# Attention scores as two 128-row matmuls, and the head of the expert layers on VectorE alone

## The chip, the cores and the metric

The kernel runs on one core of a Trainium2 chip. A core has five engines that run side by side and wait for each other through semaphores: TensorE (PE in the profile, with PEld for the loading of its stationary operand), VectorE (DVE), ScalarE (ACT), GpSimd (POOL) and SyncE (SP), which here only starts transfers. The metric is the time of one execution on the device, in microseconds (us), lower is better; the median of three executions before the change is 2091.71 us (2089.07 to 2093.18).

## What is computed

Two blocks run one after the other on one sequence of 256 rows of 1024 values. The change touches only the first block, two layers of attention and routed experts:

```python
def first_block(x, ...):
    for layer in range(2):
        mixed = mixer_dilated(x, ...) if layer == 0 else mixer_stick_breaking(x, ...)
        x = layer_norm(ALPHA * x + mixed, ln1_g[layer], ln1_b[layer])
        ffn = moe_ffn(x, router_w, router_b, exp_w_gate[layer], ...)
        x = layer_norm(ALPHA * x + ffn, ln2_g[layer], ln2_b[layer])

def moe_ffn(x, ...):
    scores = sigmoid(x @ router_w)                       # 16 experts in 4 groups
    biased = (scores + router_b).reshape(T, 4, 4)
    group_score = top_k(biased, 2)[0].sum(-1)            # the two best of a group
    best_group = argmax(group_score, axis=-1)            # one group for each token
    ...                                                  # its two best experts, gates
    y = sum over experts of gate * (silu(x @ w_gate[e]) * (x @ w_up[e])) @ w_down[e]
```

Both attentions have 16 heads of 64 values. The dilated one has three sets of q, k and v and a softmax over each; the other ("stick-breaking") has one set, a logarithm and a running sum instead of the softmax. The second block (feed-forward, a mixture of four mixers, feed-forward, twice) is unchanged.

## The kernel before

**Two-part numbers.** A matmul takes its operands in a rounded format. To keep accuracy, the kernel splits nearly every operand into a high and a low part (`split`, lines 235 to 237: ScalarE copies to the rounded format, VectorE subtracts) and adds three products (`mm3`, lines 239 to 243). Weights come as pieces of 128 by 1024 (`raw`), are split into `whi` and `wlo`, and go to TensorE.

**Attention scores.** For a score, q·k over 64 values, `stack_q` (line 535) puts the high part of q in 64 partitions of the tile `qs` and the low part in the other 64. `stack_k` (line 542) copies the high part of k into both halves of `ks` (ScalarE, then a GpSimd copy, line 547), and writes the low part of k to half the partitions of another tile, `kl` (VectorE, line 546). `score` (line 549) issues two products into one sum: all 128 partitions of `qs` with `ks` (high·high and low·high at once), then 64 partitions of `qs` with `kl`. `dilated` (line 564) runs 8 pairs of heads; `project` makes q, k, v of a pair while `attention` of the pair before it is worked off piece by piece, 4 units (2 heads, 2 blocks of rows) with 3 scores each, over 128 or 256 keys. `stick` (line 666) runs 8 pairs with `project(hp)`, `weights(hp - 1)`, `values(hp - 2)` in each round, 4 scores for each round and head pair.

**The head of an expert layer.** `attention_out` (line 427) forms the output of attention for the two blocks of 128 rows (c = 0 and 1), normalizes each (`layer_norm`, line 407) and makes the router's logits. For c = 1 the normalization's last steps go to ScalarE (line 422) and GpSimd (line 423). `moe` (line 830) then chooses the group of each token with small VectorE steps: `sc`, `bi` (lines 852, 853), the six pair sums `pr` (line 859), maxima `gs`, `gx`, `val`, `vx` and the choice `og` (line 872). TensorE counts tokens of each group (`og` with `ones_r` and `tri_r`), VectorE takes the largest count `ci` and each token's `rank`, and `places` (line 1017) makes the 0/1 matrix `P`. `xparts` (line 1020) splits x into `xsh` and `xsl`, with GpSimd doing the subtractions (argument True of `split`). `gather(k)` (line 895) multiplies P with a piece of 128 columns of x, so that each group's tokens stand together; `XTh` and `XTl` (lines 914, 915) take the result out of PSUM. After gather(0) all engines load `ci` and branch (lines 903, 904): the long body of `overflow` runs only where a group has more than 128 tokens, and is jumped over here. Then follow gather(1) to gather(7) and `experts` (line 767), 16 experts with 3 MB of weights each.

**What sets the order.** A scheduler places the instructions of each engine, by the order of the program and its own estimates; `manual_schedule` holds an engine to the written order, `issue_after` holds a piece of the program back until a given instruction. Pieces of the first expert's weights are split by `ready = list(self.parts(raws[0, 0], (2, 3)))` (line 893): pieces 2 and 3 on GpSimd.

Of the kernel before, what the change touches and what calls it, by code (L numbers as in the profile page):

```python
# [165 lines left out]
class Net:  # L166
# [240 lines left out]
    def layer_norm(self, z, gb, y, pin=False, pool=False):  # L407
# [10 lines left out]
        for s in self.halves:  # L418
            keep(nc.vector.scalar_tensor_tensor(out=y[:, s], in0=z[:, s], scalar=m[:, 0:1], in1=gb[0][:, s], op0=OP.subtract, op1=OP.mult))
        for s in self.halves:  # L420
            if pool:
                nc.scalar.activation(y[:, s], y[:, s], AF.Copy, scale=m[:, 2:3])
                self.end = nc.gpsimd.tensor_tensor(out=y[:, s], in0=y[:, s], in1=gb[1][:, s], op=OP.add)
            else:
                self.end = nc.vector.scalar_tensor_tensor(out=y[:, s], in0=y[:, s], scalar=m[:, 2:3], in1=gb[1][:, s], op0=OP.mult, op1=OP.add)
                keep(self.end)
# [58 lines left out]
    def toeplitz(self, pool, dr):  # L485

        nc = self.nc
        rel = pool.tile([32, 16], F32, name="rel", bufs=1)
        oh = pool.tile([32, 384], F32, name="oh", bufs=1)
# [4 lines left out]
        f = pool.tile([16, 384], F32, name="relf", bufs=1)  # L494
# [65 lines left out]
    def dilated(self, c1):  # L560
        nc, A = self.nc, self.A
        with self.tc.tile_pool(name="dil", bufs=1) as sp, self.tc.tile_pool(name="dr", bufs=1, space=bass.MemoryType.DRAM) as dr:
# [17 lines left out]
            def project(hp, out):  # L580
                qs, ks = (sp.tile([128, 3, 2, 256], F32R, name=n, bufs=2) for n in ("qs", "ks"))
                kl = sp.tile([128, 3, 256], F32R, name="kl", bufs=2)
                v = sp.tile([128, 2, 384], F32, name="v", bufs=2)
                out += [qs, ks, kl, v]
                for g in range(3):
                    w = w0 if hp == g == 0 else self.wload(A["dqk"][hp, g])
                    for s in range(2):
                        p = self.psB()
                        self.proj_b(p[:, :256], w[s], 0, 128, xT)
                        if s == 0:  # L590
                            self.stack_q(p, qs[:, g], lambda t: halves(t)[:, :, ::-1], halves)
                        else:
                            self.stack_k(p, ks[:, g], kl[:, g])
# [12 lines left out]
            def scores(hp, hh, qt, qs, ks, kl):  # L606
# [5 lines left out]
                for g in range(3):  # L612
                    self.score(pv[:, g, :n], qs[:, g], ks[:, g], kl[:, g], hh, q, n)
                s = sp.tile([128, 768], F32, name="s", bufs=2)
                mx = sp.tile([128, 4], F32, name="mx", bufs=4)
# [7 lines left out]
            def attention(hp, qs, ks, kl, v):  # L623
# [3 lines left out]
                for i in range(6):  # L627
                    if i < 4:
                        ready.append(scores(hp, *units[i], qs, ks, kl))
                        yield  # L630
# [39 lines left out]
    def stick(self, x):  # L670
        nc, A = self.nc, self.A
        with self.tc.tile_pool(name="sb", bufs=1) as sp:
# [25 lines left out]
            def project(hp):  # L698
                w = self.wload(A["sqk"][hp])
                qs, ks = (sp.tile([128, 2, 256], F32R, name=n, bufs=3) for n in ("qs", "ks"))  # L700
                kl = sp.tile([128, 256], F32R, name="kl", bufs=3)
                for s in range(2):
# [4 lines left out]
                    else:  # L707
                        self.stack_k(p, ks, kl)
# [7 lines left out]
                return qs, ks, kl  # L716

            def weights(qs, ks, kl):

                ps = [self.psA()[:, :384] for _ in range(2)]  # L720
                for hh, t in enumerate(ps):
                    self.score(t[:, :256], qs, ks, kl, hh, slice(128, 256), 256)
                    self.score(t[:, 256:], qs, ks, kl, hh, slice(0, 128), 128)
# [106 lines left out]
    def moe(self, x, l):  # L830
# [3 lines left out]
        with self.tc.tile_pool(name="moe", bufs=1) as sp, self.psum(512) as self.pa:  # L834
# [17 lines left out]
            v.tensor_scalar(sc, sc, 0.5, 0.5, op0=OP.mult, op1=OP.add)  # L852
# [915 lines left out]
```

## Time and profile before

| | |
|---|---|
| median of three executions | 2091.71 us |
| the profiled execution, and its span | 2091.95 us, 2090.2 us |
| PE busy | 1989.7 us (95%) |
| DVE busy | 1398.5 us (67%) |
| ACT busy | 1060.3 us (51%) |
| POOL busy | 200.6 us (10%) |
| dilated attention | about 0 to 326 us |
| head of the first and second expert layer | about 354 to 383 and 689 to 715 us |
| stick-breaking attention | about 540 to 660 us |

The profile records one execution with a start and a duration of every instruction. A busy PE is not one that works at its peak: two matmuls in a row overlap, and the time from one's start to the next one's start says more than the duration of one. The granted clock of TensorE is given as a share of full speed: 1.0 is 2.4 GHz, 0.5 is 1.2 GHz.

### The profile page before, as it was taken

To read this page: it belongs to the slowest core of one execution; us is meant where nothing else is said; L and a number is where in the kernel's file an instruction comes from. 1 tells how busy PE (TensorE), PEld (TensorE's weight loads), DVE (VectorE), ACT (ScalarE), POOL (GpSimd) and SP (SyncE) were. 2 spreads that over 40 slices of the span, in tenths; PEclk is the share of its full clock that TensorE was granted. 3 is DMA by queue.
4 is the path that set the end of the run, shared out by engine and by line. 5 is a ranking of instruction groups with operands and counts; after the bars stand their busy time and mean duration, and the time that the engine had idled before them with its cause. 6 is when DMAs were issued, how large, how long until landed. Compare 5 with 4: busy or idle time off the path is not lost. (4 is left out here: it accounts for less than half of the span.)

```text
span 2090.2 us, 38200 instructions
## 1 busy us (share of the span) xinstructions
PE 1989.7 (95%) x15106; PEld 1756.7 (84%) x15106; DVE 1398.5 (67%) x2521; ACT 1060.3 (51%) x2014; POOL 200.6 (10%) x243
## 2 busy tenths in 40 slices
PE   8999997899899699899998999999999999999998
PEld 7999996677787577699987887999899878988997
DVE  6667666788787788875566666555655576646554
ACT  5555554577565477554461334444544442335443
POOL 1212222000121200000003100000000021010000
PEclk9999998899999799999999999999999999999999
DMA  8334334698433698655543222555555543215553
GB/s 282 121 122 152 122 122 151 242 327 315 143 129 101 230 326 299 223 194 190 183 161 107 83 81 99 194 187 186 182 187 187 172 145 94 92 61 164 189 182 111
DMA packets 102528, 357.21 MB, mean 171 GB/s; under 512 B 11888, under 2 KB 15136, under 8 KB 102208
## 3 DMA queue, kind: packets, MB, share of 16 engines
q1 hardware_dynamic: 97584, 341.70, 48.8%
q10 hardware_dynamic: 4704, 12.81, 1.9%
q8 instruction: 121, 1.98, 0.4%
q14 instruction: 71, 0.58, 0.1%
q0 software_dynamic: 48, 0.13, 0.0%
HBM read 353.53 MB, written 1.07 MB: 170 GB/s over the span
## 5 line engine op out<-in xcount | busy, mean ns | idle before, releaser
L237 DVE TENSOR_TENSOR wlo<-raw,whi 128x512 fp32r<-128x512 f32 (+2 forms) x1038 | 768.3, 768 | 391.5 <-ACT whi L236 387.4
L236 ACT ACTIVATE whi<-raw 128x512 fp32r<-128x512 f32 (+2 forms) x1046 | 665.1, 667 | 607.1 <-issue 203.5
L241 PE MATMUL psB<-xTh,whi 128*128 128x256 f32 x1792 | 508.4, 284 | 8.9 <-ACT whi L236 8.3
L243 PE MATMUL psB<-xTh,wlo 128*128 128x256 f32 x1792 | 506.0, 282 | 0.2 <-DVE wlo L237 0.2
L242 PE MATMUL psB<-xTl,whi 128*128 128x256 f32 x1792 | 505.5, 282 | 0.7 <-DVE xTl L237 0.6
L241 PEld LDWEIGHTS psB<-xTh,whi 128*128 128x128 f32 x1792 | 338.8, 189 | 16.4 <-ACT whi L236 8.5
L242 PEld LDWEIGHTS psB<-xTl,whi 128*128 128x128 f32 x1792 | 339.1, 189 | 5.7 <-DVE xTl L237 1.8
L243 PEld LDWEIGHTS psB<-xTh,wlo 128*128 128x128 f32 x1792 | 339.5, 189 | 1.4 <-DVE wlo L237 0.7
L243 PE MATMUL psA<-whi,hl 128*128 128x512 f32 x352 | 139.8, 397 | 0.0
L241 PE MATMUL psA<-whi,hh 128*128 128x512 f32 x352 | 138.7, 396 | 0.0
L242 PE MATMUL psA<-wlo,hh 128*128 128x512 f32 x352 | 138.4, 393 | 0.0
L241 PE MATMUL psA<-xTh,whi 128*128 128x256 f32 (+1 forms) x352 | 105.9, 302 | 0.4 <-ACT vt L528 0.4
L241 PE MATMUL psB<-whi,XTh 128*128 128x512 f32 x256 | 103.6, 405 | 0.0
L243 PE MATMUL psA<-xTh,wlo 128*128 128x256 f32 (+1 forms) x352 | 103.3, 294 | 0.0
L242 PE MATMUL psA<-xTl,whi 128*128 128x256 f32 (+1 forms) x352 | 102.3, 291 | 0.7 <-DVE xTl L237 0.7
L243 PE MATMUL psB<-whi,XTl 128*128 128x512 f32 x256 | 101.1, 395 | 0.0
L242 PE MATMUL psB<-wlo,XTh 128*128 128x512 f32 x256 | 100.9, 394 | 0.0
L237 DVE TENSOR_TENSOR dlo<-raw,dhi 128x1024 fp32r<-128x1024 f32 (+1 forms) x68 | 80.3, 1188 | 19.5 <-ACT dhi L236 18.9
L241 PE MATMUL psB<-whi,xTh 128*128 128x384 f32 (+2 forms) x256 | 90.1, 352 | 3.3 <-ACT xTh L236 1.5
L243 PE MATMUL psB<-whi,xTl 128*128 128x384 f32 (+2 forms) x256 | 88.2, 345 | 0.3 <-DVE xTl L237 0.3
L242 PE MATMUL psB<-wlo,xTh 128*128 128x384 f32 (+2 forms) x256 | 87.9, 344 | 0.0
L292 POOL TENSOR_TENSOR ss<-ss,mh 128x1 f32<-128x1 f32 x14 | 9.5, 679 | 786.2 <-DVE ss L291 781.4
(431 smaller groups left out, 3455.3 us busy)
## 6 DMA issues: line engine op xcount, KB each, us to landing
raw<-in_egu_dram SPq DMA_DIRECT2D x128, 512.0 KB, 8.0
raw<-in_ffn1gu_dram SPq DMA_DIRECT2D x88, 512.0 KB, 3.7
raw<-in_ffn2gu_dram SPq DMA_DIRECT2D x88, 512.0 KB, 3.7
raw<-in_edn_dram SPq DMA_DIRECT2D x64, 512.0 KB, 6.7
raw<-in_dqk_dram SPq DMA_DIRECT2D x46, 512.0 KB, 3.8
raw<-in_ffn1dn_dram SPq DMA_DIRECT2D x44, 512.0 KB, 3.6
raw<-in_ffn2dn_dram SPq DMA_DIRECT2D x44, 512.0 KB, 3.7
raw<-in_wb_dram SPq DMA_DIRECT2D x40, 512.0 KB, 3.8
```

The lines of the kernel that those rows point to most:

```text
L236: self.hi = self.nc.scalar.activation(hi, src, AF.Copy)
L237: return (self.nc.gpsimd if pool else self.nc.vector).tensor_tensor(out=lo, in0=src, in1=hi.bitcast(F32), op=OP.subtract)
L241: mm(out, a[0], b[0], start=start, stop=False)
L242: mm(out, a[0], b[1], start=False, stop=False)
L243: mm(out, a[1], b[0], start=False, stop=stop)
L292: nc.gpsimd.tensor_tensor(out=ss[:, 3:4], in0=ss[:, 2:3], in1=self.mh[:, :1], op=OP.pow)
```

## The change

Scores: `ks` gets a second plane, for the low part of k. VectorE writes it where ScalarE wrote the high part, one GpSimd copy takes both planes to the other 64 partitions, and `score` issues two products over all 128 partitions with the same `qs`. `kl` is gone; the second product now holds low·low as well.

Head: the second half of `layer_norm` for c = 1 is kept as two functions (`self.steps`), and `moe` calls them between its own steps, both on VectorE. `xparts` splits only c = 0; c = 1 is split half by half inside a VectorE piece with a fixed order. `split` no longer uses GpSimd there, and the splitting of the first expert's weights, now all on VectorE, is held back behind the last of these steps. Small tiles (`rel`, `oh`, `relf`, `mx`) share memory with others.

```diff
-    def layer_norm(self, z, gb, y, pin=False, pool=False):
+    def layer_norm(self, z, gb, y, pin=False, late=False):
...
+        if late:
+            self.steps = scale, shift
+        else:
+            for f in (scale, shift):
+                for s in self.halves:
+                    keep(f(s))
...
-    def stack_k(self, p, ks, kl):
+    def stack_k(self, p, ks):
+
         for h, a, b in self.lanes:
-            self.nc.scalar.activation(ks[a, h, :], p[a, :256], AF.Copy)
+            self.nc.scalar.activation(ks[a, h, 0, :], p[a, :256], AF.Copy)
         for h, a, b in self.lanes:
-            self.nc.vector.tensor_tensor(out=kl[a, :], in0=p[a, :256], in1=ks[a, h, :].bitcast(F32), op=OP.subtract)
-            self.nc.gpsimd.tensor_copy(ks[b, h, :], ks[a, h, :].bitcast(F32))
-
-    def score(self, out, qs, ks, kl, h, q, n):
-        r = self.lanes[h][1]
-        self.mm(out, qs[:, h, q], ks[:, h, :n], True, False)
-        self.mm(out, qs[r, h, q], kl[r, :n], False, True)
+            self.nc.vector.tensor_tensor(out=ks[a, h, 1, :], in0=p[a, :256], in1=ks[a, h, 0, :].bitcast(F32), op=OP.subtract)
+            self.nc.gpsimd.tensor_copy(ks[b, h, :, :], ks[a, h, :, :].bitcast(F32))
+
+    def score(self, out, qs, ks, h, q, n):
+        for i in range(2):
+            self.mm(out, qs[:, h, q], ks[:, h, i, :n], i == 0, i == 1)
...
+            xs = self.xparts(x)
...
+            with self.tc.manual_schedule(engines={mybir.EngineType.DVE}):
...
+                tt(out=ogr, in0=val, in1=vx[:, :, None].to_broadcast([128, 2, 4]), op=OP.is_equal)
+                og8 = ogr.bitcast(F32).rearrange("p c g -> p (c g)")
+                scale(h0)
...
+                self.places(P[:, 0], rank[:, 0:4])
+                self.places(P[:, 1], rank[:, 4:8])
+                shift(h0)
+                self.split(xs[1][0][:, h0], xs[1][1][:, h0], x[1][:, h0])
+                scale(h1)
+                shift(h1)
+                placed = self.split(xs[1][0][:, h1], xs[1][1][:, h1], x[1][:, h1]).ins
             Pf = P.bitcast(F32)
-            placed = self.end.ins
-            xs = self.xparts(x)
             with self.tc.issue_after(placed):
-                ready = list(self.parts(raws[0, 0], (2, 3)))
+                ready = list(self.parts(raws[0, 0]))
```

On TensorE in the dilated attention, one unit of scores over 256 keys; `psA` is the sum, `psB` the projection of the next pair. Before:

```order
L243 MATMUL psB<-xTh,wlo 128x256
L246 MATMUL psA<-ks,qs 128x256
L246 MATMUL psA<-kl,qs 128x256
L246 MATMUL psA<-ks,qs 128x256
L246 MATMUL psA<-kl,qs 128x256
L246 MATMUL psA<-ks,qs 128x256
L246 MATMUL psA<-kl,qs 128x256
L241 MATMUL psB<-xTh,whi 128x256
```

and now:

```order
L243 MATMUL psB<-xTh,wlo 128x256
L246 MATMUL psA<-ks,qs 128x256 x6
L241 MATMUL psB<-xTh,whi 128x256
L242 MATMUL psB<-xTl,whi 128x256
L243 MATMUL psB<-xTh,wlo 128x256
```

The place among the other work is the same; the six products are now of one kind.

On VectorE in the head of the first expert layer, from the choice of the group to the branch, before:

```order
L872 TENSOR_TENSOR og<-val,vx 128x8
L237 TENSOR_TENSOR dlo<-raw_3953,dhi 128x512
L879 TENSOR_REDUCE ci<-psC 1x1
L885 TENSOR_TENSOR rank<-psC,og 128x8
L1017 TENSOR_TENSOR P<-c1t,rank 128x512 x2
L237 TENSOR_TENSOR wlo<-raw_3957,whi 128x1024
L237 TENSOR_TENSOR dlo<-raw_3955,dhi 128x512 x2
L903 TENSOR_LOAD ci
L904 COMPARE_AND_BRANCH
```

and now (L420 and L423 are the two steps of the normalization):

```order
L881 TENSOR_TENSOR og<-val,vx 128x8
L420 SCALAR_TENSOR_TENSOR x<-x,ss,row 128x512
L893 TENSOR_REDUCE ci<-psC 1x1
L895 TENSOR_TENSOR rank<-psC,og 128x8
L1030 TENSOR_TENSOR P<-c1t,rank 128x512 x2
L423 SCALAR_TENSOR_TENSOR x<-x,ss,row 128x512
L237 TENSOR_TENSOR xsl<-x,xsh 128x512
L420 SCALAR_TENSOR_TENSOR x<-x,ss,row 128x512
L423 SCALAR_TENSOR_TENSOR x<-x,ss,row 128x512
L237 TENSOR_TENSOR xsl<-x,xsh 128x512
L237 TENSOR_TENSOR wlo<-raw,whi 128x512
L917 COMPARE_AND_BRANCH
```

The weights of the first and second expert (`dlo`, `wlo`) made way for the normalization and the splits of c = 1.

On VectorE behind the branch, down to the first `XTl`, before:

```order
L994 TENSOR_TENSOR cm<-bi 128x8x3
L994 TENSOR_TENSOR cm<-bi 128x8x2
L994 TENSOR_TENSOR cm<-bi 128x8
L998 TENSOR_TENSOR rk<-c1t,cm 128x8x3
L999 COPY rk<-c1t 128x8
L915 CAST XTl<-psB 128x512
```

and now:

```order
L237 TENSOR_TENSOR wlo<-raw,whi 128x512 x7
L1007 TENSOR_TENSOR cm<-bi 128x8x3
L1007 TENSOR_TENSOR cm<-bi 128x8x2
L1007 TENSOR_TENSOR cm<-bi 128x8
L1011 TENSOR_TENSOR rk<-c1t,cm 128x8x3
L1012 COPY rk<-c1t 128x8
L928 CAST XTl<-psB 128x512
```

Seven of the eight half pieces of the first expert's weights, of which four were on GpSimd and four earlier on VectorE, now stand ahead of the first `XTl`.

## Rows read from the trace of the kernel before

**Rows 1.** Busy time by stretch: span, then each engine's busy us, clock, DMA.

```profile
core 0: us, PE busy (x) PEld busy (x) DVE busy (x) ACT busy (x) POOL busy (x), PEclk, DMA share, GB/s
100.00:200.00 100.00, 100.00 (x719) 94.38 (x718) 67.35 (x139) 54.13 (x120) 20.29 (x24) 1.00 0.43 135
...
354.00:383.00 29.00, 11.94 (x36) 9.22 (x37) 20.35 (x42) 9.54 (x18) 9.84 (x8) 0.56 0.62 228
...
420.00:440.00 20.00, 20.00 (x91) 15.92 (x90) 19.21 (x21) 16.39 (x22) 0.00 (x0) 1.00 0.88 312
...
560.00:600.00 40.00, 37.22 (x271) 33.00 (x270) 36.27 (x52) 26.90 (x49) 9.00 (x9) 1.00 0.53 172
600.00:650.00 50.00, 49.00 (x331) 41.44 (x332) 37.73 (x62) 30.64 (x57) 10.17 (x12) 1.00 0.35 117
```

**Rows 2.** Timeline of TensorE in dilated attention: start, duration, engine, line, operation.

```profile
124.62 0.38 PE L246 MATMUL psA<-kl,qs 64*128 64x256 f32 x1
124.93 0.39 PE L246 MATMUL psA<-ks,qs 128*128 128x256 f32 x1
125.24 0.38 PE L246 MATMUL psA<-kl,qs 64*128 64x256 f32 x1
125.55 0.39 PE L241 MATMUL psB<-xTh,whi 128*128 128x256 f32 x1
125.77 0.28 PE L242 MATMUL psB<-xTl,whi 128*128 128x256 f32 x1
125.89 0.29 PE L243 MATMUL psB<-xTh,wlo 128*128 128x256 f32 x1
...
128.65 0.32 PE L246 MATMUL psA<-kl,qs 64*128 64x128 f32 x1
128.90 0.33 PE L246 MATMUL psA<-ks,qs 128*128 128x128 f32 x1
```

**Rows 3.** The tile kl: loading of its stationary operand, ns min/median/max.

```profile
L246 PEld LDWEIGHTS psA<-kl,qs x128: 182/183/183, 43.1 to 651.0; 64*128 64x128 f32 x128
```

**Rows 4.** Timeline of TensorE: eight transposes of 128 columns in a row.

```profile
343.95 1.03 PE L448 MATMUL psC<-c0t,x 128*128 128x128 f32 x8
```

**Rows 5.** Timeline of GpSimd in dilated attention: one copy of line 547.

```profile
136.07 0.40 POOL L547 CAST ks<-ks 64x256 fp32r<-64x256 f32 x1
```

**Rows 6.** Timelines, head of the first expert layer, from several engines.

```profile
353.58 0.22 DVE L457 SCALAR_TENSOR_TENSOR lg<-psB,ss,br 128x16 f32<-128x16 f32 x1
354.25 2.49 POOL L423 TENSOR_TENSOR x<-x,row 128x512 f32<-128x512 f32 x2 [0.83 <-ACT x L422]
356.81 3.63 DVE L859 TENSOR_TENSOR pr<-bi 128x24 f32<-128x24 f32 x3
364.55 0.15 DVE L872 TENSOR_TENSOR og<-val,vx 128x8 fp32r<-128x8 f32 x1
366.14 1.29 DVE L1017 TENSOR_TENSOR P<-c1t,rank 128x512 fp32r<-128x512 f32 x2
370.38 0.35 DVE L994 TENSOR_TENSOR cm<-bi 128x24 f32<-128x24 f32 x3 [0.61 <-DVEq L904]
374.10 0.69 DVE L915 CAST XTl<-psB 128x512 fp32r<-128x512 f32 x1 [3.19 <-PEq L904]
374.15 0.60 ACT L914 ACTIVATE XTh<-psB 128x512 fp32r<-128x512 f32 x1 [13.73 <-PEq L904]
383.09 0.40 PE L241 MATMUL psB<-whi,XTh 128*128 128x512 f32 x1
```

**Rows 7.** Timelines, head of the second expert layer.

```profile
706.97 0.69 DVE L915 CAST XTl<-psB 128x512 fp32r<-128x512 f32 x1 [1.63 <-PEq L904]
715.13 0.40 PE L241 MATMUL psB<-whi,XTh 128*128 128x512 f32 x1
```

**Rows 8.** Line 904: TensorE's two branches, ns min/median/max, first and last start.

```profile
L904 PEldq COMPARE_BRANCH  x2: 3612/4530/5448, 368.5 to 703.2; - x2
```

**Rows 9.** Busy time by stretch: the first gathers behind the branch, columns as in Rows 1.

```profile
374.10:379.40 5.30, 5.28 (x13) 4.19 (x14) 2.51 (x8) 2.39 (x4) 0.00 (x0) 0.50 0.99 389
```

More of the change, by code (lines that the diff above doesn't have):

```diff
@@ L417, in layer_norm, with scale, shift @@
         self.rstd(m[:, 1:2], m[:, 2:3], 1.0, LN_EPS)
[L418 to L426, printed above, removed]
+        def scale(s):
+            return nc.vector.scalar_tensor_tensor(out=y[:, s], in0=z[:, s], scalar=m[:, 0:1], in1=gb[0][:, s], op0=OP.subtract, op1=OP.mult)
+        def shift(s):
+            self.end = nc.vector.scalar_tensor_tensor(out=y[:, s], in0=y[:, s], scalar=m[:, 2:3], in1=gb[1][:, s], op0=OP.mult, op1=OP.add)
+            return self.end
+        if late:
[4 more added lines that the diff above has]
+                    keep(f(s))
         return m
@@ L884, in moe @@
-            rank = sp.tile([128, 8], F32, name="rank")
-            tt(out=rank, in0=rp[:, :8], in1=og8, op=OP.mult)
-            P = sp.tile([128, 2, 4, 128], F32R, name="P")
-            for c in range(2):
-                self.places(P[:, c], rank[:, c * 4:c * 4 + 4])
+            scale, shift = self.steps
+            h0, h1 = self.halves
+            with self.tc.manual_schedule(engines={mybir.EngineType.DVE}):
+                pr = sp.tile([128, 8, 6], F32, name="pr")
+                o = 0
+                for d in (1, 2, 3):
+                    first = tt(out=pr[:, :, o:o + 4 - d], in0=b4[:, :, :4 - d], in1=b4[:, :, d:], op=OP.add)
+                    o += 4 - d
+                gs = sp.tile([128, 8], F32, name="gs")
+                v.tensor_reduce(out=gs, in_=pr, axis=AX.X, op=OP.max)
+                g2 = gs.rearrange("p (c g) -> p c g", c=2)
+                gx = sp.tile([128, 2], F32, name="gx")
+                v.tensor_reduce(out=gx, in_=g2, axis=AX.X, op=OP.max)
+                val = sp.tile([128, 2, 4], F32, name="val")
+                for c in range(2):
+                    v.scalar_tensor_tensor(out=val[:, c, :], in0=g2[:, c, :], scalar=gx[:, c:c + 1], in1=self.wt8[:, :4], op0=OP.is_equal, op1=OP.mult)
+                vx = sp.tile([128, 2], F32, name="vx")
+                v.tensor_reduce(out=vx, in_=val, axis=AX.X, op=OP.max)
+                ogr = sp.tile([128, 2, 4], F32R, name="og")
+                tt(out=ogr, in0=val, in1=vx[:, :, None].to_broadcast([128, 2, 4]), op=OP.is_equal)
+                og8 = ogr.bitcast(F32).rearrange("p c g -> p (c g)")
+                scale(h0)
+                t = self.psC()
+                for c in range(2):
+                    self.mm(t[:, :4], self.ones_r, ogr[:, c, :], c == 0, c == 1)
+                rp = self.psC()
+                self.mm(rp[:, :8], self.tri_r, ogr.rearrange("p c g -> p (c g)"), True, False)
+                self.mm(rp[:, 4:8], self.ones_r, ogr[:, 0, :], False, True)
+                ci = sp.tile([1, 1], I32, name="ci")
+                v.tensor_reduce(out=ci, in_=t[0:1, 0:4], axis=AX.X, op=OP.max)
+                rank = sp.tile([128, 8], F32, name="rank")
+                tt(out=rank, in0=rp[:, :8], in1=og8, op=OP.mult)
+                P = sp.tile([128, 2, 4, 128], F32R, name="P")
+                self.places(P[:, 0], rank[:, 0:4])
[5 more added lines that the diff above has]
+                placed = self.split(xs[1][0][:, h1], xs[1][1][:, h1], x[1][:, h1]).ins
```

72 lines of the change are left out of this document (22 added, 50 removed).

## The prediction

> **What bounds the kernel now.** I read the busy times by stretch first, because the change touches three kinds of stage with different limits. In dilated attention TensorE is busy all the time at the full clock, VectorE two thirds of it, the DMA less than half [rows 1]: TensorE bounds it. In stick-breaking attention both are near the limit: TensorE 37.2 and VectorE 36.3 of 40 us, then 49.0 and 37.7 of 50 us. In the experts TensorE is full with VectorE at 19.2 of 20 us. The head of an expert layer is the opposite: from 354 to 383 us TensorE is busy 11.9 of 29 us, at half clock, and a chain of short VectorE steps, GpSimd steps and a branch sets the time.
>
> Then I read the timeline of TensorE, for the time from start to start. Plain projection matmuls of 256 columns follow each other every 0.12 us (125.77 to 125.89). Where 64-row and 128-row scores alternate, a step is 0.31 us at 256 columns and 0.25 us at 128 (128.65 to 128.90), and the first projection matmul behind them still takes 0.22 us [rows 2]. The excess, 0.19 us, is the loading of a stationary operand, 0.183 us [rows 3]: it hides behind the running matmul in a chain of one kind, and lies open where the number of rows changes.
>
> **The change, part by part: scores.** All products become 128-row. At 256 columns I take the projection's step, the same shape: 0.12 us. At 128 columns no such product stands in the trace: 0.107 us by the transposes ((1.03 - 0.28 for the last, as a 256-column matmul shows) / 7 [rows 2, 4]), or less, down to 0.06 us, half of the 256-column step. I take the transposes, which also load a 128 by 128 operand each time.
>
> A unit over 256 keys has six products: 6 x (0.31 - 0.12) + 0.10 for the step behind them = 1.2 us. A unit over 128 keys: 6 x (0.25 - 0.107) = 0.86 us, leaving the step behind it against the first one, which is already short. There are 8 pairs x 2 = 16 of each: 33 us of TensorE time (38 us with 0.06). I take 31, because behind the last projection a softmax and not TensorE sets the pace for a few us. VectorE at 67% has room: the same work in nine tenths of the time makes 75%.
>
> In stick-breaking attention a round has eight products, four of each width: 4 x 0.19 + 4 x 0.143 = 1.33 us, and 8 rounds make 10.7 us. VectorE, at 36.3 of 40 us, will not follow all of it, and the change makes that worse: the GpSimd copy now holds two planes, 0.80 us instead of 0.40 [rows 5], 16 times here and 48 times before, 6.4 and 19 us more. While GpSimd runs, VectorE is held up: three sums of 24 values took 3.63 us while GpSimd's 128x512 steps ran, against 0.15 us for a step of that size [rows 6]. I take 6 of the 10.7 us; the ends are 0 and 10.7.
>
> GpSimd's copy now also waits for VectorE's low part. Behind it in GpSimd's queue stands the next bias sum of dilated attention or the mask sum of stick-breaking; who waits for those is the score's VectorE step. Between the stacking of the third k and its first score the program has the whole v product, 48 matmuls, 5.8 us at 0.12 us each, against some 2 us for two subtractions and two copies, so I put this wait at nothing. In the last round of stick-breaking there is no projection to cover it: one wait of up to 1.6 us (two copies), inside the 4.7 us that I left there.
>
> **The head.** VectorE's chain from the logit to `og` took 364.70 - 353.58 = 11.1 us, most of it behind GpSimd steps (354.25 to 364) [rows 6]. Now no GpSimd step is there except the root of the variance: 12 short VectorE steps at some 0.2 us with a ScalarE step between make about 2.6 us. That is 8.5 us less. The logit itself can be 0.7 us earlier, since a normalization step of that length (half of 1.29 us as the nearest row) is no longer ahead of it. So `og` is done at about 355.5 instead of 364.7.
>
> From there VectorE has more to do ahead of the first `XTl`. `og` to `P` 1.4 us (364.70 to 366.14), `P` 1.3, then two shifts, one scale and two subtractions at 0.65 to 0.7 us, 3.4 in all; each subtraction waits for a ScalarE copy, 0.60 us as `XTh`, 1.3 with the handover; one `wlo` 0.65; the branch 0.6; seven `wlo` 4.5; the short steps 0.55. Sum: 14.3 us, so the first `XTl` starts at about 369.8 against 374.10: 4.3 us earlier. In the second layer it was at 706.97, with the rest of the head 334.4 us later than in the first: there the gain is 2.9 us [rows 6, 7].
>
> Is TensorE there in time? Its gather(0) ends when the first half of `xsl` of c = 1 is done, near 361 us, and its branch takes 3.6 to 5.4 us [rows 8], to 365 or 366. So its branch, which ended last before, is hidden, and VectorE's list is late next. TensorE does gather(1) and (2) ahead of `XTl`, at half clock (at which 13 records fill 5.3 us [rows 9]), then waits some 3 us for the buffers and does five gathers, the first two or three at half clock. From `XTl` to the first expert matmul took 9.0 and 8.2 us before; I put 8.3 on it now. The gain is then 5 us in the first layer and 3 in the second.
>
> VectorE enters the experts with more undone: the first piece of expert 1 and four half pieces of `dlo`, 1.2 + 2.6 us, that before lay ahead of the branch. With 19.2 of 20 us busy in the early experts it catches up slowly. Their cover is the five buffers of split weights; if it is gone, TensorE stands for up to these 3.8 us in each layer. I take 0.5 us each. The head is worth 7 us; the ends are 0 (all given back) and 9.
>
> **Sum.** 31 + 6 + 7 = 44 us off the profiled 2091.95 us: 2048 us. That execution is 0.24 us from the median of 2091.71, so nothing is added. The small tiles that share memory cost nothing: their transfers lie at the start, with the first projections.
>
> **A rule against the scores' part.** What the rows show is that a 64-row product in this chain costs 0.31 us a step, more than a 128-row one. The Trainium skill ("TensorEngine Tiling (Array Packing)", Theoretical Speedup) promises up to twice the speed for a contraction of 64 rows or fewer in 64-row tiles, which speaks against widening the second product; the same page (Key Properties) says that a change of the tiling mode drains the engine, and by that the trace agrees (0.183 us of loading left open). By the first rule a 64-row product would cost no more than a 128-row one, widening it would win nothing, and the head alone would be left, 2085 us; no row here shows two 64-row products side by side.
>
> **Rivals.** *VectorE gives the rest back* (18%): stick-breaking gains nothing, since VectorE is its bound with GpSimd's longer copies, and the backlog eats the head: 2092 - 31 = 2061 us. For it: 36.3 of 40 and 19.2 of 20 us; against it, TensorE still was full in 600 to 650. The Trainium skill ("SBUF — State Buffer", Who interferes with whom) says that VectorE and GpSimd share a port pair by an exclusive lock and the loser blocks fully; by that rule, the trace agrees with the 3.63 us above.
> *More than forecast* (12%): 0.06 us at 128 columns, all of stick-breaking and of the head: 38 + 12 + 9 = 59, some 2033 us.
> *The open loading is not from the change of rows* (6%), but from these tiles or their sums: the scores keep 0.31 us, the head alone remains: 2085 us. Against it: a score next to a projection on the same buffers pays only at the change.
> *Slower* (3%): GpSimd's copies become the bound of the scores. The place is the wait of the first score for the copy of both planes. Each of the 32 stackings (24 and 8) would have to hold TensorE by more than 44 / 32 = 1.4 us on top of its cover, with 1.5 us each the time is 2096 us. It decides from copies of over 2.5 us each (the 5.8 us of cover, less 0.85 for subtraction, halved), against 0.80.
>
> **How the numbers follow.** The forecast has 61%, with 2041 to 2056 us as its own range (stick 0 to 10.7, head 4 to 9). The range 2034 to 2066 takes in the first rival and the edge of the second. What a measurement can tell from no change is 0.2%, 4 us. Faster: 61 + 18 + 12 and half of the 6, where the head's gain is left: 0.94. Within 0.2%: 0.03. Slower: 0.03.
>
> **What would show it.** Scores in the timeline: steps of 0.12 us without the 0.31. Dilated attention ending near 295 instead of 326 us. `pr` in under 0.5 us, and the first `XTl` released by VectorE's own `wlo` and no longer by TensorE's branch. Stick-breaking at over 95% VectorE if the first rival holds; gaps on TensorE ahead of the second expert if the backlog tells. Wrong would be the whole if the score steps stay above 0.2 us.

## The result and the profile after

The changed kernel takes 2057.37 us (median of four executions, 2051.39 to 2061.2) against 2092.02 us before (four executions, too): a ratio of 0.9834 (95% interval 0.9807 to 0.9861), 34.65 us less. The forecast was 2048 us. The time lies inside the stated range of 2034 to 2066 us, but 1.4 us above the forecast's own range of 2041 to 2056 us: about a fifth of the expected saving is missing.

Where the time went is read from the start of the same instruction in the two traces, at five places. The fourth is the first product of the second block, whose code the change does not touch; the fifth is the end of the span.

| place (TensorE) | before, us | after, us | earlier by | gain of the stage |
|---|---|---|---|---|
| first product of the output projection, first layer | 320.06 | 295.42 | 24.6 | dilated attention 24.6 |
| first score of stick-breaking | 568.45 | 537.63 | 30.8 | head and experts 6.2 |
| last product of `whi` with `yTh` in the output projection, second layer | 681.28 | 649.45 | 31.8 | stick-breaking 1.0 |
| first product of the second block | 1069.50 | 1034.54 | 35.0 | head and experts 3.1 |
| end of the span | 2090.2 | 2049.6 | 40.6 | second block 5.6 |

The 5.6 us of the last row are no effect of the change: this profiled execution was the fastest of the four, and the second block scatters by itself (last section). The 35.0 us ahead of it are the change, and they fit the 34.65 us of the medians. Forecast was 31, 5, 6 and 3 us, less 0.5 in each layer.

Busy time of the changed kernel by stretch: a piece of dilated attention, and stick-breaking from its first score to just behind its last (columns as in Rows 1).

```profile
core 0: us, PE busy (x) PEld busy (x) DVE busy (x) ACT busy (x) POOL busy (x), PEclk, DMA share, GB/s
100.00:200.00 100.00, 98.41 (x771) 97.17 (x771) 76.73 (x156) 58.60 (x131) 30.09 (x30) 1.00 0.48 148
537.63:619.40 81.77, 73.14 (x534) 65.52 (x533) 67.42 (x101) 50.85 (x93) 22.72 (x21) 0.94 0.42 139
```

and stick-breaking before:

```profile
568.45:650.97 82.52, 78.73 (x533) 66.56 (x531) 67.88 (x101) 50.47 (x93) 20.14 (x21) 1.00 0.40 133
```

Dilated attention is no longer all TensorE (98.4 instead of 100 us, against [rows 1]). Stick-breaking is nearly as long as before though TensorE is busy 5.6 us less, and TensorE's granted clock there, 1.00 before, is 0.94. VectorE is busy 82% of the stage in both kernels.

**Dilated attention.** TensorE around one unit of scores over 256 keys, after (timeline):

```profile
191.73 0.78 PE L246 MATMUL psA<-ks,qs 128*128 128x128 f32 x6
192.34 0.34 PE L241 MATMUL psB<-xTh,whi 128*128 128x256 f32 x1
...
195.48 0.95 PE L246 MATMUL psA<-ks,qs 128*128 128x256 f32 x6
196.27 0.60 PE L519 MATMUL psC<-c0t,s 128*128 128x128 f32 x4
197.36 0.88 PE L246 MATMUL psB<-v,pt 128*128 128x64 f32 x6 [0.49 <-ACT pt L532]
```

The alternation of [rows 2] is gone: six products of 128 columns take 0.61 us here (191.73 to 192.34), six of 256 columns 0.79 us. Over all 16 units of each width the mean is 0.72 and 0.90 us, against 1.42 and 1.81 us before. But behind them there is now a wait that was not there: the product with v starts 0.49 us late, for ScalarE's copy `pt`. ScalarE's queue has two other jobs ahead of that copy (timeline of ScalarE):

```profile
195.36 0.63 ACT L236 ACTIVATE whi<-raw 128x512 fp32r<-128x512 f32 x1 [1.64 <-issue]
196.02 0.77 ACT L549 ACTIVATE ks<-psB 64x256 fp32r<-64x256 f32 x2
196.81 0.49 ACT L532 ACTIVATE pt<-psC 128x384 f32<-128x384 f32 x1
```

From the first start to the last end the three take 1.9 us, about as long as the slow scores took; whether those used to cover them is tested below. TensorE's waits from 60 to 296 us, by what ended them (total us, times, longest us); before, there was none from 40 us on:

```profile
PE psB L246 <- ACT pt L532: 2.8, 6, 0.5
PE psB L246 <- DVE pt L534: 0.9, 1, 0.9
PE psC L519 <- ACT pt L532: 0.2, 1, 0.2
```

**Stick-breaking.** Eight scores now fill one row of 1.03 us. What became of the time is seen at the first values. Before, and then after (timeline of TensorE):

```profile
579.16 0.87 PE L742 MATMUL psC<-c0t,z 128*128 128x128 f32 x6 [0.51 <-ACT z L734]
```

```profile
544.24 1.03 PE L246 MATMUL psA<-ks,qs 128*128 128x256 f32 x8
548.20 1.54 PE L746 MATMUL psC<-c0t,z 128*128 128x128 f32 x6 [2.93 <-ACT z L738]
```

At this place VectorE and ScalarE do the same list in both kernels with the same starts, 30.96 us earlier (ScalarE's exponential at 578.26 and 547.30; VectorE's scan, before and after):

```profile
574.10 2.69 DVE L731 TENSOR_TENSOR_SCAN sc<-e,msb 128x768 f32<-128x768 f32 x1 [1.07 <-ACT e L729]
543.14 2.69 DVE L735 TENSOR_TENSOR_SCAN sc<-e,msb 128x768 f32<-128x768 f32 x1 [1.07 <-ACT e L733]
```

TensorE only arrives earlier and waits longer. And then it works at half speed; the granted clock in steps of 2 us, after:

```profile
544.00:546.00 2.00, 1.27 (x12) 1.12 (x10) 1.97 (x2) 1.08 (x2) 0.21 (x1) 1.00 0.34 133
546.00:548.00 2.00, 0.00 (x0) 0.00 (x0) 1.91 (x4) 0.70 (x1) 0.00 (x0) 0.80 0.00 0
548.00:550.00 2.00, 1.80 (x9) 1.80 (x10) 1.91 (x5) 1.94 (x5) 0.48 (x1) 0.50 0.00 0
550.00:552.00 2.00, 2.00 (x11) 1.41 (x12) 1.97 (x4) 1.95 (x4) 0.93 (x3) 0.50 0.00 0
552.00:554.00 2.00, 2.00 (x13) 1.67 (x10) 2.00 (x2) 0.62 (x2) 1.91 (x1) 0.50 0.67 219
554.00:556.00 2.00, 2.00 (x19) 2.00 (x19) 2.00 (x2) 0.55 (x2) 0.00 (x0) 0.99 0.36 107
```

In these rows VectorE is busy 11.8 of 12 us. A second fall comes near 615 us, behind a wait of 1.95 us for GpSimd's copy of `ks`:

```profile
614.89 0.39 PE L246 MATMUL psA<-ks,qs 128*128 128x256 f32 x1 [1.95 <-POOL ks L552]
```

Before, the clock is 1.00 in all of the stage.

Followed through the whole stage, VectorE keeps the lead of 30.9 to 31.2 us with which it came in, but for one step, down to 577 us (after); it is busy 23.5 of 24 us from 544 to 568. Behind that it is not full (3.1 of 4 us from 568 to 612) and gains: the lead is 32.1 us at 580 and 33.2 at 610. In the last round it waits for the score that waited for GpSimd's copy, and the lead falls back to 32.0 us.

**The head.** VectorE in the first expert layer after, from the second logit to the first `XTl`:

```profile
327.44 0.23 DVE L462 SCALAR_TENSOR_TENSOR lg<-psB,ss,br 128x16 f32<-128x16 f32 x1 [0.40 <-PE psB L246]
...
328.41 0.35 DVE L868 TENSOR_TENSOR pr<-bi 128x24 f32<-128x24 f32 x3
...
329.82 0.17 DVE L881 TENSOR_TENSOR og<-val,vx 128x8 fp32r<-128x8 f32 x1
...
337.51 0.68 DVE L237 TENSOR_TENSOR wlo<-raw,whi 128x512 fp32r<-128x512 f32 x1
340.96 4.30 DVE L237 TENSOR_TENSOR wlo<-raw,whi 128x512 fp32r<-128x512 f32 x7 [2.76 <-DVEq L917]
...
345.61 0.68 DVE L928 CAST XTl<-psB 128x512 fp32r<-128x512 f32 x1
```

Against [rows 6], `pr` takes 0.35 instead of 3.63 us and `og` is done 2.5 us after the logit's start instead of 11.1. But the branch now costs VectorE 2.76 us. The branch's records on VectorE and TensorE (ns min/median/max, first and last start):

```profile
L917 DVEq COMPARE_BRANCH  x2: 63/68/72, 337.8 to 665.9; - x2
L917 PEldq EVENT_SEMAPHORE  x2: 51/51/51, 339.5 to 667.6; - x2
L917 DVEq EVENT_SEMAPHORE  x2: 21/21/21, 340.8 to 668.9; - x2
```

VectorE's comparison is at 337.8, its first record behind it at 340.8, 3.0 us later; before, it took 3.1 us (367.2 to 370.3). TensorE was through at 339.5 and waits for VectorE:

```profile
340.92 1.22 PE L246 MATMUL psA<-P,xsh 128*128 128x512 f32 x2 [5.31 <-DVEq L917]
...
345.35 0.85 PE L246 MATMUL psA<-P,xsl 128*128 128x512 f32 x2
346.03 0.39 PE L241 MATMUL psB<-whi,XTh 128*128 128x512 f32 x1
...
346.49 0.63 PE L246 MATMUL psA<-P,xsh 128*128 128x512 f32 x2
```

The first expert product at 346.03 no longer stands behind all gathers: the order now mixes the two.

### The profile page after: what moved, and what is told of

Same layout as the page of the kernel before. It is cut to its first block, busy times and chain, and to the rows that moved or that the text cites. A ratio compares the mean times of both kernels' runs of the same rounds, so it can differ in the third digit from the quotient of the medians.

```text
span 2049.6 us, 38189 instructions
## 1 busy us (share of the span) xinstructions
PE 1949.6 (95%) x15106; PEld 1734.2 (85%) x15106; DVE 1398.3 (68%) x2541; ACT 1054.6 (51%) x2010; POOL 192.0 (9%) x223
## 5 line engine op out<-in xcount | busy, mean ns | idle before, releaser
L237 DVE TENSOR_TENSOR wlo<-raw,whi 128x512 fp32r<-128x512 f32 (+2 forms) x1046 | 779.0, 773 | 389.0 <-ACT whi L236 378.1
```

The lines of the kernel that those rows point to most:

```text
L237: return (self.nc.gpsimd if pool else self.nc.vector).tensor_tensor(out=lo, in0=src, in1=hi.bitcast(F32), op=OP.subtract)
```

## The experiments

All twelve in one table. "Out 1" is the first product of the output projection in the first layer, "stick" the time from the start of the first score product in stick-breaking to the start of the last, "block 2" the first product of the second block. The first 60 us, with the loads and the first waits, differ from run to run by up to 1.8 us for the same code (3.5 in one) and move everything behind them, so "block 2" is to be read with "out 1". Each ratio is against the kernel before as it was executed beside that run, with medians from 2092.02 to 2099.87 us: ratios compare better than medians.

| run | median, us | ratio to before (95%) | out 1 | stick | block 2 |
|---|---|---|---|---|---|
| before | 2092.02 | | 320.06 | 82.52 | 1069.50 |
| after | 2057.37 | 0.9834 (0.9807 to 0.9861) | 295.42 | 81.66 | 1034.54 |
| scores alone | 2063.53 | 0.9860 (0.9816 to 0.9904) | 294.98 | 81.85 | 1041.43 |
| head alone | 2081.81 | 0.9945 (0.9921 to 0.9969) | 320.12 | 81.78 | 1060.56 |
| mirrored order | 2079.35 | 0.9935 (0.9910 to 0.9959) | 311.68 | 80.66 | 1059.79 |
| values later | 2061.74 | 0.9827 (0.9789 to 0.9865) | 298.94 | 81.14 | 1041.81 |
| zero half plane | 2059.15 | 0.9812 (0.9767 to 0.9858) | 296.99 | 79.64 | 1034.24 |
| copies on ScalarE | 2055.55 | 0.9794 (0.9750 to 0.9839) | 295.66 | 78.66 | 1030.99 |
| dilated only | 2065.70 | 0.9841 (0.9797 to 0.9885) | 295.60 | 84.36 | 1036.13 |
| weights first | 2057.30 | 0.9807 (0.9758 to 0.9855) | 297.26 | 81.43 | 1036.70 |
| unread products | 2058.62 | 0.9812 (0.9780 to 0.9845) | 296.55 | 85.84 | 1040.15 |
| three together | 2054.35 | 0.9785 (0.9753 to 0.9816) | 296.73 | 80.81 | 1037.46 |
| exchanged copies | 2062.62 | 0.9833 (0.9800 to 0.9865) | 295.22 | 81.83 | 1039.20 |
| two together | 2059.11 | 0.9818 (0.9791 to 0.9844) | 296.99 | 76.86 | 1032.84 |

Of the whole times that the expectations named, the first three runs came within 3 us, and the copies on ScalarE missed by 0.6 us. The other seven with a forecast came out later than expected, values later by 11 us, dilated only by 7, two together by 7; the rest by 1 to 5. The whole time holds the scatter of the second block (last section), so the theories are judged by the stages.

**Do the parts add?** The scores' hunks of the diff on the old head, and the head's hunks on the old scores.

> The score part alone, on the old head. Theory (the two parts add): dilated attention ends some 25 us earlier as in the changed kernel, stick-breaking gains about 1 us, the head nothing: about 2066 us. Rival (the score part only pays because the new head takes up what it frees, or the reverse): within 4 us of 2057 or of 2092.

> The head part alone, on the old scores. Theory (GpSimd was holding VectorE and its steps stood in the chain): the pair sums take 0.35 us for three instead of 3.63, og comes 8 to 9 us earlier after the logit, the end of the first block 8 to 9 us earlier: about 2083 us. Rival (the backlog of weight splits takes it back): og early all the same, but the first block ends within 2 us of before, 2090 to 2092 us.

Both as the first theory had it. The scores bring the second block 28.1 us forward, the head 8.9 us, together 37.0 against 35.0 for both. In the head alone `pr` takes 0.35 us, in the scores alone, with the old head and its GpSimd steps, 3.63 us as before: the head's change made it fast, not the scores'. The backlog does not eat the head.

**Is it the change of rows?** The kernel before, with every second score in the other order:

```diff
     def score(self, out, qs, ks, kl, h, q, n):
         r = self.lanes[h][1]
-        self.mm(out, qs[:, h, q], ks[:, h, :n], True, False)
-        self.mm(out, qs[r, h, q], kl[r, :n], False, True)
+        self.turn = not getattr(self, "turn", False)
+        pair = [(qs[:, h, q], ks[:, h, :n]), (qs[r, h, q], kl[r, :n])][::1 if self.turn else -1]
+        for i, (a, b) in enumerate(pair):
+            self.mm(out, a, b, i == 0, i == 1)
```

> The kernel before, with the two products of every second score in the other order, so that two 64-row products and two 128-row products stand side by side and a unit has four changes of row count instead of six; same products, same operands. Theory (the open loading belongs to the change of row count): 32 units of dilated attention save 2 x 0.14 to 0.19 us each, 9 to 12 us, and stick-breaking next to nothing: about 2081 us; a product behind one of its own kind starts 0.12 us after it. Rival (it belongs to the 64-row product or to this tile): every step stays at 0.25 to 0.31 us, 2090 to 2094 us.

```profile
206.21 0.38 PE L246 MATMUL psA<-kl,qs 64*128 64x256 f32 x1
206.52 0.51 PE L246 MATMUL psA<-ks,qs 128*128 128x256 f32 x2
206.95 0.50 PE L246 MATMUL psA<-kl,qs 64*128 64x256 f32 x2
207.38 0.39 PE L246 MATMUL psA<-ks,qs 128*128 128x256 f32 x1
```

A step across a change takes 0.31 us (206.21 to 206.52); two products of one kind and the change behind them 0.43 us, for 128 rows (206.52 to 206.95) and for 64 rows (206.95 to 207.38) alike, so the second of a kind adds 0.12 us. The same products in another order end dilated attention 8.4 us earlier (9 to 12 expected; the loads at the start took 1.3 of it), and the second block starts 9.7 us earlier. This is shown: the open 0.19 us belongs to the change of row count. A 64-row product behind its like is as dear as a 128-row one, neither slower nor cheaper.

**Why did stick-breaking gain nothing?** First, values one round later, so that the chain from score to `z` has more time:

```diff
-                for hp in range(10):
+                for hp in range(11):
...
-                    if hp >= 2:
-                        values(hp - 2, z.pop(hp - 2))
+                    if hp >= 3:
+                        values(hp - 3, z.pop(hp - 3))
```

> The changed kernel, with the values of a pair of heads taken one round later in stick-breaking (three buffers for z). Theory (after the change the chain score, exponential, logarithm, scan, exponential, transpose is what TensorE waits for, 8.5 us of idle time between the first and the last score, and the clock falls to half in such a wait): the idle time falls below 4 us, the clock stays at 1.00, and stick-breaking is 6 to 10 us shorter: 2047 to 2051 us. Rival (VectorE, busy 67.4 of 81.8 us, and GpSimd's longer copies set the pace): within 2 us of the changed kernel's 2057 us.

The theory fell. The wait for `z` went and another one stood in the same place:

```profile
553.51 0.55 PE L241 MATMUL psB<-xTh,whi 128*128 128x256 f32 x1 [3.40 <-DVE qs L543]
```

with the clock at 0.50 behind it, 10.2 us of idle time instead of 8.6, and VectorE 3.8 to 4.0 of each 4 us from 552 to 564. So the chain is not the cause by itself; at this place the rival, VectorE's full list, has it. Next, less work for GpSimd and less for VectorE:

```diff
-            self.nc.gpsimd.tensor_copy(ks[b, h, :, :], ks[a, h, :, :].bitcast(F32))
+            self.nc.gpsimd.tensor_copy(ks[b, h, 0, :], ks[a, h, 0, :].bitcast(F32))
```

(with `ks` in tiles that stay, whose other half plane is zeroed once), and

```diff
     def evac(self, out, in_):
...
-        if self.ev % 2:
+        if self.ev % 2 or getattr(self, "on_act", False):
```

(with `on_act` true in stick-breaking).

> The changed kernel, with the other half of the second plane of ks set to zero once, in tiles that stay (low times low is left out, as in the kernel before), so that GpSimd copies one plane again (0.40 instead of 0.61 us) and does not wait for VectorE's low part. Theory (the longer copies cost little: TensorE sets the pace in dilated attention, VectorE's own list in stick-breaking): dilated attention unchanged within 0.5 us, stick-breaking 1 to 3 us shorter, mostly the 1.95 us wait of its last round: 2054 to 2057 us. Rival (GpSimd's longer copies hold VectorE and ate the 10 us of stick-breaking): 6 us or more shorter there, 2051 us or less.

> The changed kernel, with every PSUM copy of stick-breaking attention that alternated between ScalarE and VectorE on ScalarE: VectorE is rid of 8 copies of 0.55 us for pts and 4 for v. Theory (VectorE's list sets the pace of stick-breaking after the change): the stage is 3 to 5 us shorter and TensorE idles less between the first and the last score than 8.5 us: 2052 to 2055 us. Rival (the chain from score to value, whichever engine works on it): within 1 us of the changed kernel.

With GpSimd's copy back at 0.40 us the stage is 2.0 us shorter, all of it in the last round: the wait for `ks` there is 1.02 instead of 1.95 us, and the clock stays at 1.00 behind it. GpSimd's longer copies cost that much and not the 10 us. With VectorE rid of eight copies in the stage (and four around it) VectorE is busy 3.0 us less, the stage is 3.0 us shorter, the least that was expected, and the second block starts 3.6 us earlier, as VectorE's list would have it. The expected fall of TensorE's idle time did not come (10.0 us). Then the old scores in this stage alone (the 64-row second product and `kl`, in `stick`):

> The changed kernel with the old scores (64-row second product, one-plane copies) in stick-breaking attention alone. Theory (TensorE's saving there went into waits): the 9.6 us that its score products took less come back, the idle time falls from 8.5 to about 3.7 us, the clock stays at 1.00, and the first block ends within 1.5 us of the changed kernel: 2055 to 2059 us. Rival (the saving is in the result, another cost offsets it): the first block ends 5 us or more later.

The second block starts 1.6 us later than after the full change, nearly as expected, and the idle time fell to 3.1 us. But the clock fell here too, behind a wait of 1.28 us for `z`:

```profile
549.00:551.00 2.00, 1.85 (x12) 1.55 (x12) 1.94 (x5) 1.93 (x5) 0.79 (x2) 0.74 0.00 0
551.00:553.00 2.00, 1.58 (x8) 1.35 (x8) 1.97 (x4) 1.94 (x3) 0.76 (x1) 0.50 0.00 0
553.00:555.00 2.00, 2.00 (x9) 1.86 (x9) 2.00 (x2) 0.38 (x1) 1.06 (x1) 0.50 0.76 252
...
537.45:621.82 84.37, 81.26 (x534) 69.06 (x532) 67.74 (x101) 50.36 (x93) 19.15 (x21) 0.96 0.40 130
```

TensorE's order in this stage is that of the kernel before, its idle time no longer (3.1 against 3.8 us), and the stage is 84.4 instead of 82.5 us. The head alone has that order too, with the clock at 1.00 throughout, and took 81.8 us. So with the old scores, where TensorE has little slack, one fall of the clock is worth 1.9 to 2.6 us. Whether it costs as much in the changed kernel is another question. To keep the clock up there, 20 products that nobody reads were put in the wait:

```diff
+                    if hp == 2:
+                        with self.tc.issue_after(self.last):
+                            t = self.psC()
+                            for _ in range(20):
+                                self.mm(t[:, :256], xT[0][:, 0, :128], xT[0][:, 0, :])
```

> The changed kernel with 20 products that nobody reads, of 256 columns (2.4 us at 0.12 us), on TensorE behind the scores of the second round of stick-breaking, where it idles 2.93 us. Theory (the wait's second price is the clock, which falls to 0.50 behind it for some 6 us): the clock stays at 1.00 through 545 to 556 us of the stage, which gets 2.5 to 3.5 us shorter though TensorE does more: 2053 to 2055 us. Rival (VectorE's list sets the pace in those microseconds whatever the clock): clock at 1.00, the stage as long as before within 0.7 us. Third case: the clock falls all the same, and nothing changes.

The clock held past 548 us, but the scheduler now put ScalarE's next exponential and logarithm ahead of the copy `pts`, and a new wait opened:

```profile
548.65 0.88 PE L747 MATMUL psC<-c0t,z 128*128 128x128 f32 x6 [0.70 <-ACT z L739]
...
553.21 0.86 PE L246 MATMUL psC<-pts,vs 128*64 128x256 f32 x4 [3.33 <-ACT pts L532]
```

with the clock at 0.50 from 554 us on and a stage of 85.8 us. So this run says nothing on the clock alone. Another one does, by chance. The run with weights first, told next, changes only the heads; in stick-breaking all its engines have the order of the changed kernel. It too waits for `z`, 2.67 us, but its clock does not fall there:

```profile
548.00:550.00 2.00, 0.00 (x0) 0.00 (x0) 1.87 (x5) 0.49 (x1) 0.00 (x0) 1.00 0.00 0
550.00:552.00 2.00, 1.59 (x12) 1.39 (x12) 1.94 (x4) 1.94 (x5) 0.28 (x1) 1.00 0.00 0
552.00:554.00 2.00, 1.11 (x9) 0.77 (x9) 1.94 (x5) 1.94 (x4) 0.94 (x2) 1.00 0.00 0
```

The stage takes 81.43 against 81.66 us, and TensorE idles 10.5 instead of 8.6 us. So with the new scores that fall costs 0.2 us: what TensorE does more slowly it would else have waited. The scores alone and the exchanged copies, with the same order there and the fall, took 81.8 us, so 0.2 us is no more than such runs differ by. This answers the question for this place: after the change VectorE's list sets the pace there, at either clock. (At the end of the stage, behind the wait for `ks`, the clock fell in this run too.)

**VectorE's branch.** Five of the eight half pieces of `wlo` ahead of the branch, by an order written out:

```diff
                 shift(h1)
+                with self.tc.issue_after(first.ins):
+                    next(some)
                 placed = self.split(xs[1][0][:, h1], xs[1][1][:, h1], x[1][:, h1]).ins
+                with self.tc.issue_after(first.ins):
+                    for _ in range(3):
+                        next(some)
+                rv = nc.values_load(ci[0:1, 0:1], min_val=0, max_val=256)
```

> The changed kernel with five of the eight half pieces of the first expert's low weights ahead of VectorE's branch, two of them in the gaps where it waited for ScalarE's xsh, three behind the last split, and three behind the branch. Theory (VectorE's branch takes 2.8 us when nothing is queued on the engine behind which the fetch can hide, and the others wait for it): the idle time behind it falls under 1 us, the first XTl comes 2 to 3 us earlier after the logit, gather(1) 1 to 1.5 us earlier, the first block ends 1 to 4 us earlier: 2053 to 2056 us. Rival (TensorE's own branch or the products are the limit): XTl earlier but the first expert products not, within 1 us of the changed kernel.

```profile
340.84 1.89 DVE L237 TENSOR_TENSOR wlo<-raw,whi 128x512 fp32r<-128x512 f32 x3
345.35 1.90 DVE L237 TENSOR_TENSOR wlo<-raw,whi 128x512 fp32r<-128x512 f32 x3 [2.63 <-DVEq L934]
```

The theory fell. The comparison came at 341.2, while the first of the three was running, and VectorE's first record behind it at 345.2: 4.0 us, 1.5 of them covered. So 2.63 us stay open. `XTl` came 16.9 instead of 18.2 us after the logit, but gather(1) 14.6 instead of 13.5, and the second block no earlier. Why this branch took 4.0 and not 3.0 us is open.

**The waits of dilated attention.** The alternating copies there exchanged between ScalarE and VectorE (and set back behind it):

```diff
             yT = self.new_T("yT")
+            self.ev = 1
             halves = lambda t: t.rearrange("p (c t) -> p c t", c=2)
```

> The changed kernel with the PSUM copies of dilated attention that alternate between ScalarE and VectorE exchanged. Theory (the 0.47 us that TensorE waits once in each pair of heads is ScalarE's queue: two other copies stand ahead of pt there, which the longer scores used to cover): the wait at that place is no longer for a ScalarE copy, TensorE's idle time between 40 and 295 us changes from 4.9 us by 2 us or more, one way or the other, and with it the end of dilated attention. Rival (any engine would be late there, because the scores that covered the copy are shorter): 4 to 6 us of idle time again, now for VectorE's copies.

From 60 to 285 us not one wait is left, and by 280 us TensorE was 2.7 us ahead of the changed kernel: the 0.47 us were ScalarE's queue. All of it and more was given back at the end, where the last pair has no projection beside it and VectorE is late (2.17 us for `pt`). Behind that wait the granted clock fell to 0.50, from 292 to 300 us. Out 1, which stands in the middle of the last pair's work, is at 295.2 as before the exchange, but the last product with v starts at 302.7 instead of 299.7 us. The idle time changed by 1.2 us, less than the 2 us that the theory named; the place and the cause of the wait were as it said.

**Together.** The first is the zero half plane, the copies on ScalarE and the unread products; the second the first two alone.

> The changed kernel with three edits together: the zero half plane (0.8 us in stick-breaking, 1.8 us by the end of the first block in its own run), the copies of stick-breaking on ScalarE alone (2.5 and 3.6 us), and the 20 unread products. Theory (they work on different waits and add): the first block ends 5 to 9 us earlier than in the changed kernel, about 2049 to 2053 us. Rival (all shorten the same wait): 3 to 4 us, 2054 us.

> The changed kernel with the zero half plane and with the copies of stick-breaking on ScalarE alone, without the unread products, which in their own run opened a new wait of 3.33 us behind them. Theory (the two edits work on different waits and add): stick-breaking from the first to the last score 75 to 77 us instead of 81.8, the first block's end 4 to 5.5 us earlier than in the changed kernel, about 2052 us. Rival (both shorten the same wait): 77 us or more and 3.5 us or less, 2054 us.

The 0.8 and 2.5 us that the first of them counts for the stage are 2.0 and 3.0 us from first to last score, as in the table. With the unread products nothing adds (80.8 us). Without them the stage is 76.9 us, as the theory had it: there the two edits add. But from out 1 on the first block gains only 3.3 us on the changed kernel, no more than the copies alone gave (3.8), and what the rival had: behind the last score TensorE waits 2.75 us for `z` in this run, against 0.49 us. In the whole time it does not show: 2059.11 us, and in the profiled execution the second block took 1025.4 us to the end of the span, against 1015.1 in the changed kernel's. By the medians the copies on ScalarE and the three together are lowest, at 2055.55 and 2054.35 us, but their intervals overlap with that of the changed kernel. No version is shown to beat it.

## Why the prediction was right, and where it was off

**Scores, mechanism: right.** The excess was the change of row count (mirrored order), and widening the product removes it: the alternating steps of 0.31 and 0.25 us are gone. The Trainium skill ("TensorEngine Tiling (Array Packing)", Key Properties) says that a change of the tiling mode drains the engine; by the mirrored order, 0.31 against 0.12 us, the trace agrees. The speedup that the Trainium skill gives on the same page (Theoretical Speedup) for 64 rows or fewer did not appear for a 64-row product in a chain: 0.12 us like the wide one. What two such tiles at work together would give, no run here shows.

**Dilated attention, 31 forecast, 24.6 measured: two terms of the sum.** Added up from start to start without the waits, TensorE's stretch from 40 us to out 1 went from 280.0 to 250.1 us, 29.9 instead of 33. The steps of the new products were put too short, and those of the old ones a little too long: the 192 products went from 51.7 to 25.9 us (0.12 us at 128 columns and 0.15 at 256, where 0.107 and 0.12 had been put), 25.8 us less instead of 32. The steps next to them gained 4 us instead of 1.6. The waits are the other miss: 2 us were allowed at the end, and 4.9 came, one in every pair of heads. The step that failed is "VectorE at 67% has room": it had (76.7% measured, 75 forecast), but the question was what stands ahead of one ScalarE copy in its queue.

**Stick-breaking, 6 forecast, 1.0 measured: the term was mis-sized, at the low end of its range.** With the old scores at a clock of 1.00 the stage took 82.5 and 81.8 us in two runs, with the new ones 81.4 to 81.9 in four, so it is not shown that it gained anything. Added up from start to start, the scores took TensorE 9.2 us less. The idle time took back 4.9 us (3.8 to 8.6), and the other steps, slower at half clock, 3.5 us. These are two forms of one loss: the run whose clock did not fall behind the first wait waited longer and needed as long. Down to 577 us the pace is VectorE's list, the first rival's mechanism in this stage, and taking copies off it gave 3.0 us. Not all of the stage is so: the sign that the prediction named for that rival, VectorE over 95% busy, did not come (82%), and the last round is held by GpSimd's copy, which the changed kernel made longer. How the loss splits between the two is known only from the runs with copies moved (3.0 us) and shortened (2.0 us). The step that failed is the middle value: "I take 6" was a guess between two ends, and at 545 to 555 us VectorE has no room at all.

**GpSimd.** The copy of two planes takes 0.61 us and not the doubled 0.80, and costs 2.0 us in stick-breaking, in its last round. The wait for it in the last round was 1.95 us where up to 1.6 was forecast. The rival that GpSimd would bound the scores is out.

**The head, 7 forecast, 9.3 measured with the experts, 8.9 alone: right in size, by errors that go opposite ways.** It lies about at the upper end of 9 that the prediction gave. `og` came 2.5 us after the logit (2.6 forecast). The first `XTl` gained 2.4 us on the logit instead of 4.3 less 0.7, because VectorE's branch was put at 0.6 us, the value of [rows 6], and took 2.76: there it had hidden behind 2.6 us of splits queued ahead of it, which the change moves away. The list of steps from `og` to `XTl` also adds up to 13.7 us and not to the 14.3 that was used; 15.6 were measured. The term from `XTl` to the first expert product, 8.3 us, was wrong the other way: the new order starts the products between the gathers, 0.4 us after the first `XTl`. The last gather starts 6.8 us behind the first `XTl`, instead of 8.8, with eight expert products already among the gathers. The prediction did not look at this part of TensorE's order.

**The range** held partly by luck: dilated attention and stick-breaking gave 11.4 us less than forecast, the head 2.3 us more. The first rival, all given back but 31 us, lies nearer in time than the forecast (2061 us) but is wrong in its parts: stick-breaking gave nothing, as it said, but the head gave all that it was put at, and dilated attention 24.6 and not 31 us.

## What to carry to other kernels

- Two kinds of matmul that alternate are worth a look at the time from start to start: here each change of row count cost 0.19 us at 256 columns, and a second product that does twice the arithmetic was cheaper than one that changes the shape.
- When work on the bounding engine gets shorter, list what it covered: the queue ahead of the one copy that it waits for next. Mean load says little (ScalarE is busy 59% in dilated attention now, and its copy is the wait in each pair).
- A branch that looks short in a trace may be short only for what is queued ahead of it: here it took VectorE about 3 us in both kernels, and showed as 0.61 us of idle time before and 2.76 us after.

## What was not expected of the hardware

TensorE's clock fell to half behind waits in stick-breaking, but not by a rule that one could read off the wait: it fell behind 1.28 us in one run and 2.93 us in another, and held behind 2.67 us in a third, whose order there is that of the second. What it costs depends on who sets the pace: 1.9 to 2.6 us where TensorE has little slack, 0.2 us where it waits for VectorE anyway.

The second block, with the same products in the same order but for at most four of 9168, took between 1009.6 and 1025.4 us from its first product to the end of the span, in the fourteen profiled executions. Its first 150 us, after and with the two edits together:

```profile
1034.54:1184.54 150.00, 141.59 (x2267) 126.72 (x2267) 104.33 (x237) 55.93 (x127) 25.56 (x37) 0.98 0.34 114
...
1032.84:1182.84 150.00, 140.82 (x2203) 125.11 (x2204) 100.40 (x229) 54.05 (x122) 25.68 (x37) 0.92 0.33 106
```

The clock was 0.98 in one and 0.92 in the other, and TensorE did 2203 products instead of 2267 in the same time. What sets it off is open. It is why gains of 2 to 4 us in the first block cannot be read from the whole time, and why the stages were compared instead.
